# A two-level Strassen kernel: when the additions for later operands are queued

## The chip, the cores and the metric

One core of a Trainium2 chip. The metric is the device time of one execution in microseconds; the median of three runs is 793.61 (793.61 to 793.72). All times below are in microseconds unless marked otherwise.

## The reference

With a depth of one, the reference is a single gated short-convolution layer on a sequence of 1024 tokens of width 1024:

```
u = rms_norm(x, pre_norm)
z, bg, cg, v = split(u @ w_in, 4)              # w_in 1024 x 8192, four parts of 2048
y = bg * causal_dwconv(cg * v, conv_w) * silu(z)   # 3 taps over the tokens, per channel
m = y @ w_out                                  # w_out 2048 x 1024
out = x + rms_norm(m, post_norm)
```

Everything is float32.

## The kernel before

**Products.** Each float32 matrix product is made on TensorE from a rounded high part and a rest (`split`: ScalarE copies the high part, VectorE subtracts it to get the low part), as low x high, high x low and high x high. On top of that lies Strassen's scheme in Winograd's form: a 2 x 2 block product takes seven products, called a, b, c, e, d, f and g in the order in which they are issued, in place of eight. The operands of the products are sums of blocks. A product of u with w_in is `product(p, i)`: 12 matmuls of 512 columns into a bank of PSUM. Products a, c, d and g of a pair accumulate in one bank (`px`), e and f in another (`pv`). What a bank holds after a, c and e is copied to SBUF by ScalarE (`snap`, L196) before the next product adds to it, and VectorE adds the copies to later states (`after`: L215 for d, giving `sne`, L220 for f, giving `snc`).

**Pairs.** The 2048 channels go in 16 chunks of 128. Chunk c has two pairs of blocks of w_in: pair p = 2c (cg and v) and pair p = 2c + 1 (z and bg). So pairs run from 0 to 31, and the main loop does the slots of pairs 2 to 31. From pair 6 on (`DEEP = 3` chunks are done without it) product b is itself taken apart once more: the small products a' to g' work on 256 columns, and lie between the large ones. Their left operands c', e', d' and g' are sums of quarters of the operand of b. They are made once: `deep_parts(k)` puts high and low part of block k together again (L618, one addition on GpSimd for each k), `deep_subs(k)` makes four subtractions on GpSimd (L624 to L627), and `deep_split` splits one of the four sums into high and low (two ScalarE copies and two VectorE subtractions of 256 columns; `ucl_deep`, `u_b`, `udl_deep` and `ugl_deep` are the subtractions' outputs). c' is first needed behind f of pair 6.

**Beside the products.** In each pair GpSimd makes the four sums of w_in's blocks for the next pair (`add_s`: L146, L148, L142, L150), the sums for the small products (`deep_sums`, L650 to L654) and products with the gates (L217, L223, L225). VectorE makes the low parts (all at L155: `wcl` is the low part of the operand of product c), the additions after each product, and the convolution (`conv`, L583, started by `start_conv` behind g of an even pair for the first chunks, later behind d'). After f of an odd pair ScalarE takes the SiLU of `snc` (L222), after g' that of `sna` (L793).

**w_out.** The last product, y with w_out, also goes by Strassen's scheme, and the sums of w_out's blocks are made ahead of it in eight of the pairs: `fetch_t(j)` loads four blocks of 128 x 512 behind product c of the pair (L276), `add_t` subtracts them in four dependent steps on VectorE (L281 to L284) and stores each to DRAM (L286, `t_d`). `TODO` says which pair does which j. In an even pair this stands behind product d, in an odd one behind g.

**What sets the order.** The schedule is manual: every engine runs its instructions in the order in which the code issues them. One loop goes through the slots, and for each one issues the product, then `prepare` (the splits for products that start within 7.0 units; a large product counts 2.72 and a small one 0.72), then `after`, then loads, sums and the extras of that slot, last of them what the table `UNDER` names for it. All DMAs are issued by SP, which also runs in order. 36 pages of 2 KB for each partition hold all passing tiles.

Of the kernel before, what the change touches and what calls it, by code (L numbers as in the profile page):

```python
# [16 lines left out]
DEEP = 3  # L17
# [4 lines left out]
def kernel(  # L22
# [16 lines left out]
    nc = tc.nc  # L39
# [31 lines left out]
    def page(name, dtype=F32, shape=(HB,)):  # L71

        return pages.tile([P, *shape], dtype, tag="pg", name=name, bufs=PAGES)
# [58 lines left out]
    def block(p, n, k):  # L132
        return flat(raws[p, n, k])
# [19 lines left out]
    def split(src, hi, lo):  # L153
        nc.scalar.copy(hi, src)  # L154
        nc.vector.tensor_sub(lo, src, hi.bitcast(F32))  # L155
# [21 lines left out]
    def product(p, i, ks=None):  # L177

        w = wt[p, i]
        which = {"b": "y", "e": "v", "f": "v"}.get(i, "x")  # L180
        first = i in "abe"
        if first and (p, which) not in banks:
            banks[p, which] = bank(f"p{which}_{p}")
        ps = banks[p, which]
        for k in range(KH) if ks is None else ks:
            hi, lo = (h[:, k * P : (k + 1) * P] for h in w)
            last = k == KH - 1
            nc.tensor.matmul(ps, lo, UH[i][:, k], start=first and k == 0, stop=False, skip_group_check=True)  # L188
            nc.tensor.matmul(ps, hi, UL[i][:, k], start=False, stop=False, skip_group_check=True)  # L189
            nc.tensor.matmul(ps, hi, UH[i][:, k], start=False, stop=last, skip_group_check=True)  # L190
# [55 lines left out]
    def fetch_s(c):  # L246

        if c >= CH:
            ts = [page(f"s{e}_{c}") for e in (0, 1)]
            for e in (0, 1):  # L250
                nc.sync.dma_start(ts[e], y_d[:, c - CH, e * HB : (e + 1) * HB])
            done[c] = done[c], *ts
# [17 lines left out]
    ts = {}  # L270

    def fetch_t(j):

        ts[j] = [page(f"t{n}_{j}") for n in range(4)]
        for n, t in enumerate(ts[j]):
            nc.sync.dma_start(t, wov[:, j + n // 2 * CH, n % 2 * HB : (n % 2 + 1) * HB])  # L276

    def add_t(j, eng):

        t = ts.pop(j)  # L280
        eng.tensor_sub(t[1], t[1], t[0])  # L281
        eng.tensor_sub(t[3], t[3], t[1])
        eng.tensor_sub(t[0], t[3], t[0])
        eng.tensor_sub(t[2], t[2], t[3])  # L284
        for n in range(4):
            nc.sync.dma_start(t_d[:, n, j], t[n])  # L286


# [325 lines left out]
    def deep_parts(ks):  # L614

        for k in ks:
            deep[k] = page(f"deep{k}")
            nc.gpsimd.tensor_add(deep[k], UH["b"][:, k].bitcast(F32), UL["b"][:, k].bitcast(F32))  # L618

    def deep_subs(ks):  # L620

        for k in ks:
            (b11, b12), (b21, b22) = ((t[:, :HH], t[:, HH:]) for t in (deep[k], deep[k + KQ]))
            nc.gpsimd.tensor_sub(b12, b12, b11)  # L624
            nc.gpsimd.tensor_sub(b22, b22, b12)
            nc.gpsimd.tensor_sub(b11, b22, b11)
            nc.gpsimd.tensor_sub(b21, b21, b22)  # L627
# [3 lines left out]
    def deep_split(i):  # L631

        k0, l0 = DEEP_U[i]
        ls = slice(l0, l0 + HH)
        if i != "e'":
            deep[i] = [tmp.tile([P, KQ, HH], F32R, tag="ub", name=f"u{i[0]}{h}_deep", bufs=6) for h in "hl"]
        for k in range(KQ):
            if i == "e'":
                hi, lo = UH["b"][:, k, ls], UL["b"][:, k, ls]
            else:  # L640
                hi, lo = (t[:, k] for t in deep[i])
            split(deep[k0 + k][:, ls], hi, lo)

    def deep_sums(c, part):

        (a11, a12), (a21, a22) = ((t[:, :HH], t[:, HH:]) for t in (block(p, 0, 1) for p in (2 * c, 2 * c + 1)))
        t = page(f"ds{part}_{c}")
        deep[c, part] = t
        if part == 0:
            nc.gpsimd.tensor_add(t[:, :HH], a21, a22)  # L650
            nc.gpsimd.tensor_sub(t[:, HH:], t[:, :HH], a11)
        else:
            nc.gpsimd.tensor_sub(t[:, :HH], a11, a21)
            nc.gpsimd.tensor_sub(t[:, HH:], a12, deep[c, 0][:, HH:])  # L654
# [17 lines left out]
    def deep_product(c, i):  # L672

        n, off = DEEP_W[i]
        which = {"b'": "y'", "e'": "v'", "f'": "v'"}.get(i, "x'")
        first = i in ("a'", "b'", "e'")
        if first:
            banks[c, which] = bank(f"p{which[0]}2_{c}")
        ps = banks[c, which][:, :HH]
        for k in range(KQ):  # L680
            hi, lo = (h[:, off + k * P : off + (k + 1) * P] for h in deep_w[c, n])
            if i in deep:
                uh, ul = (t[:, k] for t in deep[i])
            else:
                kk, l0 = {"a'": (k, 0), "b'": (k + KQ, 0), "e'": (k, HH), "f'": (k + KQ, HH)}[i]
                uh, ul = (u["b"][:, kk, l0 : l0 + HH] for u in (UH, UL))
            nc.tensor.matmul(ps, lo, uh, start=first and k == 0, stop=False, skip_group_check=True)  # L687
            nc.tensor.matmul(ps, hi, ul, start=False, stop=False, skip_group_check=True)  # L688
            nc.tensor.matmul(ps, hi, uh, start=False, stop=k == KQ - 1, skip_group_check=True)  # L689
# [5 lines left out]
    def deep_after(c, i):  # L695
        which, row, half = DEEP_C[i]
        t = sn[2 * c + row, "a"][:, half * HH : (half + 1) * HH]
        nc.vector.tensor_add(t, banks[c, which][:, :HH], t)
        if i == "d'":
            start_conv(c)  # L700
# [34 lines left out]
        OP[side, i, h] = t  # L735

    END = len(PAIRS) - 1
    TODO = {p: j for j, p in enumerate([4, 8, 10, 12, 14, 16, 15, 17])}

    slots = [("a", 2), ("b", 2)]  # L740
    for p in range(2, len(PAIRS)):
# [14 lines left out]


    UNDER = {
        ("c", 2 * DEEP - 1): lambda: deep_parts([0, 2]),
        ("e", 2 * DEEP - 1): lambda: deep_parts([1, 3]),  # L760
        ("d", 2 * DEEP - 1): lambda: deep_subs([0]),
        ("f", 2 * DEEP - 1): lambda: deep_subs([1]),
        ("a", 2 * DEEP): lambda: deep_split("c'"),
        ("g", 2 * DEEP - 1): lambda: deep_split("e'"),
        ("c", 2 * DEEP): lambda: deep_split("d'"),
        ("e", 2 * DEEP): lambda: deep_split("g'"),
    }


    at, t = [], 0.0  # L770
# [6 lines left out]
    def prepare(n):  # L777
        while ready[0] < len(slots) and at[ready[0]] < at[n + 1] + LEAD:
            i, p = slots[ready[0]]
            if i[1:]:  # L780
                deep_prep(p, i)
            elif (p, i) not in wt:
                split_w(p, i)
            ready[0] += 1

    first_chunk("")
    for n, (i, p) in enumerate(slots):
        if i[1:]:
            deep_product(p, i)
            prepare(n)  # L790
            deep_after(p, i)
            if i == "g'":
                nc.scalar.activation(sn[2 * p + 1, "a"], sn[2 * p + 1, "a"], AF.Silu)  # L793
            continue
        product(p, i)
        prepare(n)
        after(p, i)
        q, prev = p + 1, p // 2 - 1
        if p == 2:
            first_chunk(i)  # L800
        if i == "c":
            if p % 2 and p // 2 < DEEP:
                nc.scalar.activation(sn[p, "a"], sn[p, "a"], AF.Silu)
            if p in TODO:
                fetch_t(TODO[p])
            if p % 2 == 0 and p > 2:
                fetch_s(prev)
            if p % 2 == 0 and p // 2 >= DEEP:
                deep_sums(p // 2, 1)
        elif i == "e":  # L810
            add_s(q, "ec")
        elif i == "d":
            if p + 2 <= END:
                fetch(p + 2)
            add_s(q, "d")
            if p in TODO and p % 2 == 0:
                add_t(TODO[p], nc.vector)
            if p % 2 == 0 and p > 2:
                add_y(prev)
        elif i == "f":  # L820
            add_s(q, "f")
            if p == 2:
                add_y(0)
        elif i == "g":
            if p in TODO and p % 2:
                add_t(TODO[p], nc.vector)
            if p % 2 and q <= END and q // 2 >= DEEP:
                deep_sums(q // 2, 0)
        if DEEP < NC and (i, p) in UNDER:
            UNDER[i, p]()  # L830
        if p == END - 1 and i in "cd":
            fetch_unit()
        if p == END and i in "acdg":
            split_unit()
            fetch_unit()
# [153 lines left out]
```

## Time and profile before

| | |
|---|---|
| median of three runs | 793.61 |
| the profiled execution | 793.75 |
| its span, first to last instruction | 791.9 |
| mean granted TensorE clock | 0.999 |
| busy: TensorE, weight loads, VectorE | 780.0, 654.0, 601.7 |
| busy: ScalarE, GpSimd | 335.6, 360.8 |
| pairs 2 to 31, c of pair 4 at | 103.52 |
| c of pairs 5, 6, 7, 8 at | 122.56, 139.47, 161.85, 180.36 |
| c of pairs 14, 16, 18 at | 293.70, 331.48, 370.22 |

PE is TensorE, PEld its weight loads, DVE VectorE, ACT ScalarE, POOL GpSimd, SP SyncE. A row of the timeline gives the start, the duration, the engine, the line and the operation, the written and the read tiles with their shapes, and in brackets how long the engine was idle in front of it and what ended that. A row of waits gives who waited for whom: the total, the number and the longest. A row of windows gives a stretch, its length, and the busy time of PE, PEld, DVE, ACT and POOL with the number of instructions, then the granted clock, the DMA share and GB/s.

### The profile page before, as it was taken

To read this page: it belongs to the slowest core of one execution; us is meant where nothing else is said; L and a number is where in the kernel's file an instruction comes from. 1 tells how busy PE (TensorE), PEld (TensorE's weight loads), DVE (VectorE), ACT (ScalarE), POOL (GpSimd) and SP (SyncE) were. 2 spreads that over 40 slices of the span, in tenths; PEclk is the share of its full clock that TensorE was granted. 3 is DMA by queue.
4 is the path that set the end of the run, shared out by engine and by line. 5 is a ranking of instruction groups with operands and counts; after the bars stand their busy time and mean duration, and the time that the engine had idled before them with its cause. 6 is when DMAs were issued, how large, how long until landed. Compare 5 with 4: busy or idle time off the path is not lost.

```text
span 791.9 us, 10797 instructions
## 1 busy us (share of the span) xinstructions
PE 780.0 (99%) x3728; PEld 654.0 (83%) x3728; DVE 601.7 (76%) x832; ACT 335.6 (42%) x610; POOL 360.8 (46%) x257
## 2 busy tenths in 40 slices
PE   9999999899999999999999999999999999999996
PEld 8888887788888888888888888888888888888885
DVE  6899757788787878798977768787878867744766
ACT  8564433333433343424242434242434547554441
POOL 2616538747474746555564737373838100000020
PEclk9999999999999999999999999999999999999999
DMA  9110451226161708182714233232415569973037
GB/s 328 46 53 16 132 199 55 80 66 200 54 220 34 241 12 282 51 284 75 226 56 145 87 114 106 95 106 93 144 57 169 190 207 393 403 276 118 0 108 264
DMA packets 108325, 114.50 MB, mean 145 GB/s; under 512 B 6584, under 2 KB 72176, under 8 KB 108272
## 3 DMA queue, kind: packets, MB, share of 16 engines
q1 hardware_dynamic: 108256, 113.82, 43.3%
q8 instruction: 29, 0.48, 0.2%
q14 instruction: 24, 0.20, 0.1%
q10 hardware_dynamic: 16, 0.00, 0.0%
HBM read 84.44 MB, written 29.36 MB: 144 GB/s over the span
## 4 chain that ended last, share of the span: by engine, by line
PE 80%; DVE 6%; POOL 5%; issue 4%; DMA 3%; ACT 2%; SPq 0%; DVEq 0%; POOLq 0%; ACTq 0%
PE px L188 12%; PE px L189 12%; PE px L190 11%; PE pv L188 6%; PE pv L189 6%; PE pv L190 6%; PE po_x L867 3%; PE po_x L865 3%; PE po_x L866 3%; PE po_v L867 2%; PE po_v L865 2%; PE po_v L866 2%; PE px L687 1%; PE px L689 1%; PE px L688 1%
## 5 line engine op out<-in xcount | busy, mean ns | idle before, releaser
L217 POOL TENSOR_TENSOR sne<-sne,cv 128x512 f32<-128x512 f32 x15 | 25.1, 1673 | 155.9 <-DVE sne L215 140.2
L907 POOL TENSOR_TENSOR acc<-acc,xr 128x512 f32<-128x512 f32 x4 | 6.4, 1592 | 132.8 <-DVE acc L906 130.9
L583 DVE SCALAR_TENSOR_TENSOR cv<-gpad,cw,cv 128x1024 f32<-128x1024 f32 x32 | 43.9, 1371 | 19.0 <-ACT cv L581 18.5
L146 POOL TENSOR_TENSOR se<-raw,raw 128x512 f32<-128x512 f32 x31 | 51.8, 1670 | 3.1 <-DMA raw<-in_sc_w_in 2.7
L150 POOL TENSOR_TENSOR sf<-raw,sc 128x512 f32<-128x512 f32 x31 | 53.1, 1711 | 0.0
L225 POOL TENSOR_TENSOR gpad<-snc,sne 128x512 f32<-128x512 f32 x15 | 20.2, 1345 | 71.1 <-DVE snc L220 71.1
L155 DVE TENSOR_TENSOR wel<-se,weh 128x512 fp32r<-128x512 f32 x31 | 50.9, 1641 | 1.4 <-ACT weh L154 1.4
L148 POOL TENSOR_TENSOR sc<-se,raw 128x512 f32<-128x512 f32 x31 | 50.0, 1614 | 2.4
L188 PE MATMUL pv<-u_f,wfl 128*128 128x512 f32 x124 | 48.6, 392 | 1.6 <-DVE wfl L155 1.3
L188 PE MATMUL px<-u_d,wdl 128*128 128x512 f32 x124 | 48.6, 392 | 0.0
L188 PE MATMUL px<-u_a,wal 128*128 128x512 f32 x124 | 48.6, 392 | 0.0
L188 PE MATMUL pv<-u_e,wel 128*128 128x512 f32 x124 | 48.6, 392 | 0.0
L196 ACT COPY sna<-px 128x512 f32<-128x512 f32 x30 | 17.5, 583 | 73.3 <-PE px L190 47.8
L188 PE MATMUL px<-u_g,wgl 128*128 128x512 f32 x124 | 48.5, 391 | 0.0
L189 PE MATMUL pv<-u_e,weh 128*128 128x512 f32 x124 | 48.6, 392 | 0.0
L189 PE MATMUL px<-u_d,wdh 128*128 128x512 f32 x124 | 48.6, 392 | 0.0
L189 PE MATMUL px<-u_a,wah 128*128 128x512 f32 x124 | 48.6, 392 | 0.0
L189 PE MATMUL px<-u_g,wgh 128*128 128x512 f32 x124 | 48.4, 390 | 0.0
L190 PE MATMUL pv<-u_f,wfh 128*128 128x512 f32 x124 | 48.3, 389 | 0.0
L189 PE MATMUL pv<-u_f,wfh 128*128 128x512 f32 x124 | 48.3, 389 | 0.0
L190 PE MATMUL px<-u_g,wgh 128*128 128x512 f32 x124 | 48.3, 389 | 0.0
L189 PE MATMUL px<-u_c,wch 128*128 128x512 f32 x124 | 48.2, 389 | 0.0
(370 smaller groups left out, 2484.1 us busy)
## 6 DMA issues: line engine op xcount, KB each, us to landing
raw<-in_sc_w_in SPq DMA_DIRECT2D x128, 256.0 KB, 4.2
y_d<-cv SPq DMA_DIRECT2D x16, 512.0 KB, 3.0
s_d<-s SPq DMA_DIRECT2D x32, 256.0 KB, 2.4
t<-in_sc_w_out SPq DMA_DIRECT2D x32, 256.0 KB, 4.3
t_d<-t SPq DMA_DIRECT2D x32, 256.0 KB, 2.3
s<-y_d SPq DMA_DIRECT2D x16, 256.0 KB, 3.9
xr<-in_x SPq DMA_DIRECT2D x16, 256.0 KB, 4.5
xa<-in_x SPq DMA_DIRECT2D x4, 512.0 KB, 5.4
```

The source lines that it names most:

```text
L146: nc.gpsimd.tensor_add(t, block(p, 1, 0), block(p, 1, 1))
L148: nc.gpsimd.tensor_sub(t, sums[p, "e"], block(p, 0, 0))
L150: nc.gpsimd.tensor_sub(t, block(p, 0, 1), sums[p, "c"])
L155: nc.vector.tensor_sub(lo, src, hi.bitcast(F32))
L188: nc.tensor.matmul(ps, lo, UH[i][:, k], start=first and k == 0, stop=False, skip_group_check=True)
L189: nc.tensor.matmul(ps, hi, UL[i][:, k], start=False, stop=False, skip_group_check=True)
L190: nc.tensor.matmul(ps, hi, UH[i][:, k], start=False, stop=last, skip_group_check=True)
L217: nc.gpsimd.tensor_mul(t, t, cvs[c][:, HB:])
L583: nc.vector.scalar_tensor_tensor(cv, gpad[:, j : j + L], tap(c, j), cv, op0=ALU.mult, op1=ALU.add)
L865: nc.tensor.matmul(ps, lo, u[:, 0, k], start=first, stop=False, skip_group_check=True)
L866: nc.tensor.matmul(ps, hi, u[:, 1, k], start=False, stop=False, skip_group_check=True)
L867: nc.tensor.matmul(ps, hi, u[:, 0, k], start=False, stop=last, skip_group_check=True)
```

## The change

`TODO` gives the w_out sums to pairs 8, 10, 12, 13, 14, 15, 16 and 17, where it was 4, 8, 10, 12, 14, 15, 16 and 17. In odd pairs the four steps no longer stand together behind g: one stands behind each of d, f, a (of the next pair, which is issued before g) and g, each with its store. In even pairs all four still stand behind d. `UNDER` has the work for the small products' operands earlier and in smaller pieces: the four additions behind c, e, d and f of pair 4 (before: two behind c and two behind e of pair 5), the subtractions behind g of pair 4 and c of pair 5 (before: d and f of pair 5), and the splits behind e, d and f of pair 5 and a of pair 6 (before: a of pair 6, g of pair 5, c and e of pair 6). The amount of work is the same.

```diff
-    def add_t(j, eng):
+    def add_t(j, steps=range(4)):
 
-        t = ts.pop(j)
-        eng.tensor_sub(t[1], t[1], t[0])
-        eng.tensor_sub(t[3], t[3], t[1])
-        eng.tensor_sub(t[0], t[3], t[0])
-        eng.tensor_sub(t[2], t[2], t[3])
-        for n in range(4):
+        t = ts[j]
+        for n, a, b in [((1, 1, 0), (3, 3, 1), (0, 3, 0), (2, 2, 3))[n] for n in steps]:
+            nc.vector.tensor_sub(t[n], t[a], t[b])
             nc.sync.dma_start(t_d[:, n, j], t[n])
...
-    TODO = {p: j for j, p in enumerate([4, 8, 10, 12, 14, 16, 15, 17])}
+    TODO = {p: j for j, p in enumerate([8, 10, 12, 13, 14, 15, 16, 17])}
...
     UNDER = {
-        ("c", 2 * DEEP - 1): lambda: deep_parts([0, 2]),
-        ("e", 2 * DEEP - 1): lambda: deep_parts([1, 3]),
-        ("d", 2 * DEEP - 1): lambda: deep_subs([0]),
-        ("f", 2 * DEEP - 1): lambda: deep_subs([1]),
-        ("a", 2 * DEEP): lambda: deep_split("c'"),
-        ("g", 2 * DEEP - 1): lambda: deep_split("e'"),
-        ("c", 2 * DEEP): lambda: deep_split("d'"),
-        ("e", 2 * DEEP): lambda: deep_split("g'"),
+        ("c", 2 * DEEP - 2): lambda: deep_parts([0]),
+        ("e", 2 * DEEP - 2): lambda: deep_parts([2]),
+        ("d", 2 * DEEP - 2): lambda: deep_parts([1]),
+        ("f", 2 * DEEP - 2): lambda: deep_parts([3]),
+        ("g", 2 * DEEP - 2): lambda: deep_subs([0]),
+        ("c", 2 * DEEP - 1): lambda: deep_subs([1]),
+        ("e", 2 * DEEP - 1): lambda: deep_split("c'"),
+        ("d", 2 * DEEP - 1): lambda: deep_split("e'"),
+        ("f", 2 * DEEP - 1): lambda: deep_split("d'"),
+        ("a", 2 * DEEP): lambda: deep_split("g'"),
     }
...
             if p in TODO and p % 2 == 0:
-                add_t(TODO[p], nc.vector)
+                add_t(TODO[p])
...
         elif i == "g":
-            if p in TODO and p % 2:
-                add_t(TODO[p], nc.vector)
             if p % 2 and q <= END and q // 2 >= DEEP:
                 deep_sums(q // 2, 0)
+        if i in "dfag" and p % 2 != (i == "a") and p - (i == "a") in TODO:
+            add_t(TODO[p - (i == "a")], ["dfag".index(i)])
```

## Prediction, made before the changed kernel was run

> **What bounds the kernel now.** I read the page, then TensorE's waits, then the busy time of each pair from the start of its product c to that of the next pair, then the timelines around the waits.
>
> ```profile
> span 791.9 us, 10797 instructions
> PE 780.0 (99%) x3728; PEld 654.0 (83%) x3728; DVE 601.7 (76%) x832; ACT 335.6 (42%) x610; POOL 360.8 (46%) x257
> ```
> ```profile
> PE px L687 <- DVE dw1l L155: 1.5, 1, 1.5
> PE pv L188 <- DVE wfl L155: 1.3, 2, 1.0
> PE pv L188 <- ACT wch L154: 0.3, 2, 0.2
> ```
> ```profile
> 103.52:122.56 19.04, 19.04 (x85) 15.77 (x84) 12.27 (x17) 4.88 (x9) 6.62 (x5) 1.00 0.74 241
> 122.56:139.47 16.91, 16.57 (x74) 13.44 (x72) 13.13 (x12) 7.58 (x13) 14.24 (x11) 1.00 0.09 25
> 139.47:161.85 22.38, 19.95 (x98) 16.26 (x96) 17.59 (x23) 8.78 (x19) 16.83 (x16) 1.00 0.32 94
> ...
> 293.70:312.97 19.27, 19.27 (x98) 16.37 (x97) 16.86 (x22) 6.85 (x12) 14.63 (x11) 1.00 0.71 231
> 312.97:331.48 18.51, 18.51 (x92) 15.63 (x90) 12.97 (x17) 7.37 (x13) 7.44 (x6) 1.00 0.29 88
> 331.48:351.18 19.70, 19.55 (x98) 16.29 (x96) 18.87 (x23) 6.22 (x11) 11.57 (x9) 1.00 0.68 235
> 351.18:370.22 19.04, 18.76 (x92) 15.55 (x90) 16.20 (x20) 7.99 (x14) 10.82 (x8) 1.00 0.43 130
> 370.22:389.90 19.68, 19.52 (x98) 16.29 (x96) 19.51 (x22) 6.23 (x11) 13.51 (x10) 1.00 0.60 201
> ```
>
> TensorE is busy for 99% of the span, so work on the other engines counts only where it makes or ends a wait of TensorE. The window rows (stretch and length, then PE, PEld, DVE, ACT, POOL, clock) are pairs 4, 5, 6 and 14 to 18. Pair 4 has seven products in 19.04, so one takes 2.72. An undisturbed even pair takes 19.27 and an odd one 18.51. Against these, pair 5 (six products, 16.32) loses 0.59, pair 6 loses 3.11, pair 16 0.43, pair 17 0.53 and pair 18 0.41. That is 3.70 around the preparation of the small products' operands and 1.37 around the odd pairs with w_out sums, 5.07 in all: the most that the change can win. A loss is some 0.25 more than its named wait: a product otherwise starts 0.16 before its predecessor's end, and after a wait it restarts some 0.1 slower.
>
> One mechanism prices everything here. It is seen ahead of product c of pair 16 (c16):
>
> ```profile
> 325.42 0.69 DVE L215 TENSOR_TENSOR sne<-px,sne 128x512 f32<-128x512 f32 x1
> 326.02 0.68 DVE L155 TENSOR_TENSOR wcl<-sc,wch 128x512 fp32r<-128x512 f32 x1
> 326.62 0.68 DVE L220 TENSOR_TENSOR snc<-pv,snc 128x512 f32<-128x512 f32 x1
> 327.22 0.41 DVE L698 TENSOR_TENSOR sna<-px,sna 128x256 f32<-128x256 f32 x1
> 329.03 0.69 DVE L155 TENSOR_TENSOR dw0l<-raw,dw0h 128x512 fp32r<-128x512 f32 x1 [1.40 <-ACT dw0h L154]
> 329.64 1.78 DVE L155 TENSOR_TENSOR wel<-se,weh 128x512 fp32r<-128x512 f32 x1
> ```
> ```profile
> 326.18 1.68 POOL L217 TENSOR_TENSOR sne<-sne,cv 128x512 f32<-128x512 f32 x1 [10.99 <-DVE sne L215]
> 327.83 1.29 POOL L142 TENSOR_TENSOR raw<-raw,raw 128x512 f32<-128x512 f32 x1
> 329.08 1.80 POOL L223 TENSOR_TENSOR cv<-snc,sne 128x512 f32<-128x512 f32 x1
> ```
> ```profile
> 327.33 0.63 ACT L222 ACTIVATE snc<-snc 128x512 f32<-128x512 f32 x1 [4.05 <-DVE snc L220]
> 327.87 0.62 ACT L793 ACTIVATE sna<-sna 128x512 f32<-128x512 f32 x1
> ...
> 329.42 0.58 ACT L196 COPY sna<-px 128x512 f32<-128x512 f32 x1
> ```
> ```profile
> 331.25 0.39 PE L190 MATMUL px<-u_g,wgh 128*128 128x512 f32 x1
> 331.48 0.39 PE L188 MATMUL px<-u_c,wcl 128*128 128x512 f32 x1
> ```
>
> VectorE and GpSimd take turns, one whole instruction each, when both work from SBUF. L217 waits for wcl and ends 1.16 after it; L223 ends 1.16 after dw0l; wel ends 0.54 after L223. An own turn is thus some 1.15 on GpSimd and 0.55 on VectorE (I take half of that at 256 columns), and an addition of 0.69 becomes up to 1.8 where it meets a GpSimd instruction. VectorE instructions that read PSUM are not held: snc takes 0.68 beside L217.
>
> The same rows give the chain that ends at c16: sne, wcl, snc, SiLU (L222), SiLU (L793), the first halves of the splits of dw0 and e, and the copy of a16's bank (L196). c16 accumulates in that bank and must wait for the copy. It ends at 330.00, c16 starts at 331.48: 1.48 of slack, and nobody waits today.
>
> The Trainium skill (SBUF — State Buffer, "SBUF: two separate sides") has a rule that speaks against single additions among GpSimd's work: the two engines share a port pair under an exclusive lock held for a whole instruction, VectorE's side only with two SBUF inputs. The rows agree (1.78 for wel), and add the order of turns, which the page doesn't state.
>
> **Part 1: pairs 13, 15 and 17 one by one.** Step n of the w_out sums now stands behind products d, f, a and g. Worked for pair 15: step t1 comes behind sne and takes wcl's free turn (326.02 to 326.71). L217 then ends at 327.86, wcl has to wait for it (328.41), and snc starts at 328.33 in place of 326.62 and ends at 329.01, 1.71 late. L142 takes its turn at 328.41 and ends at 329.56; step t3 waits for it and ends at 330.11; the sum sna (L698) behind t3 ends at 330.45 in place of 327.63. SiLU L793 needs sna: it starts at 330.48 in place of 327.87, 2.61 late, ACT's queue behind it moves as a whole, and the copy ends at 332.61. c16 starts at 332.65, 1.17 late, and with the slower restart 1.27 is lost. Three such pairs, ahead of c14, c16 and c18: 3.81.
>
> What these pairs win: before, four additions stood in front of the split wfl for f16.
>
> ```profile
> 334.37 1.23 DVE L281 TENSOR_TENSOR t<-t,t 128x512 f32<-128x512 f32 x1
> ...
> 339.51 1.77 DVE L155 TENSOR_TENSOR wfl<-sf,wfh 128x512 fp32r<-128x512 f32 x1
> ```
> ```profile
> 340.89 0.39 PE L190 MATMUL px<-u_d,wdh 128*128 128x512 f32 x1
> ```
> ```profile
> t<-in_sc_w_out SPq DMA_DIRECT2D x32, 256.0 KB, 4.3
> ```
>
> f16 was due at 341.12 (0.23 behind the last matmul of d16), wfl came at 341.28. Afterwards L223 ends at 331.27, L150 alone (1.29) at 332.5 and dw0l at 333.07. From there both queues alternate: six VectorE turns of 0.55 (wel, t0, wdl, L230, t2, wfl), four GpSimd turns of 0.58 and three of 1.15, 9.1 together, so wfl ends near 342.2. TensorE, 1.27 late, needs it at 342.4: no loss, 0.2 to spare. The waits of pairs 16 to 18 (1.37) go. SP's queue: an odd pair's loads are issued at c as before and first read two products later (over 5.4 us, against 4.3 to land). Each store waits on SP for its own step, and behind it stand only the next store, y_d and the next even pair's loads, a few tenths later; that pair's idle VectorE time (19.27 less 16.86) hides it, and without that cover it would cost about pair 16's 0.43. Pair 4 loses its additions; pair 13 has 5.5 idle on VectorE for its own (18.51 less 12.97). Sum of part 1: 3.81 less 1.37, 2.44 slower. Bounds: 1.37 faster if both steps find free turns (two at 0.60, inside the slack); 5.9 slower if each chain waits one more turn of 1.15.
>
> **Part 2: the small products' operands earlier.**
>
> ```profile
> 117.11 1.68 POOL L225 TENSOR_TENSOR gpad<-snc,sne 128x512 f32<-128x512 f32 x1 [12.42 <-DVE snc L220]
> ```
> ```profile
> 124.72 4.64 DVE L583 SCALAR_TENSOR_TENSOR cv<-gpad,cw,cv 128x1024 f32<-128x1024 f32 x2 [1.27 <-ACT cv L581]
> ...
> 134.23 0.69 DVE L220 TENSOR_TENSOR snc<-pv,snc 128x512 f32<-128x512 f32 x1 [0.75 <-PE pv L190]
> ...
> 144.23 0.63 DVE L155 TENSOR_TENSOR ucl_deep<-deep,uch_deep 128x256 fp32r<-128x256 f32 x1 [5.08 <-ACT uch_deep L154]
> ```
>
> Before, VectorE idles 5.08 until the subtractions are through, and the work behind it, dw1l last, comes late. Afterwards three of the four additions L618 fall into GpSimd's idle 12.42, which hides them (three turns of 1.15, 3.5; without that cover they would stand ahead of c6). Without pair 4's four additions, snc of f4 can start when TensorE ends f4 (103.52 plus 4 x 2.72 plus 0.16), so L225 starts at 115.4, and with L150 and the fourth L618 GpSimd is at 119.5. Eight subtractions of 0.7, two VectorE turns of 0.55 and the two L583 (1.1 each) bring it to 128.4; wfl for f5 ends at 128.9, due at 122.56 plus 3 x 2.72, 130.72. Pair 5's 0.59 goes.
>
> Then the new place costs. In alternation: L146 130.1, wal 130.6, L148 131.8, both ucl 132.4, wgl 133.0, sne 133.6, the first split of e' 133.9, L217 135.0, the second 135.3, L142 136.5, wcl 137.0, snc 137.6 in place of 134.9. From SiLU's start to the copy's end pair 15 takes 2.67; here the second SiLU isn't between them but two half-width copies of d' are, an estimate of 0.2 more: the copy of a6 ends at 140.4. c6 is due at 139.47 less 0.59, 138.88, and loses 1.6. From L223 (138.3) both queues alternate without a gap: GpSimd 1.29, 1.15, four of 0.58, three of 1.15; VectorE four of 0.28 and five of 0.55; 12.1 together, so wfl for f6 ends at 150.4. f6 is due 9.64 behind c6 (as f16 behind c16) at 150.1: it loses 0.6. c' no longer waits, since the splits are behind it. Part 2 loses 2.2 where before lost 3.7: 1.5 faster. Bounds: 3.7 faster if snc keeps its time; 0.8 slower if two more GpSimd turns come in front. Both queues' order is written out, so I take the worked value.
>
> **Sum.** 2.44 slower less 1.5 faster is 0.94 slower. The profiled execution took 793.75 (span 791.9, the rest around it) beside a median of 793.61: 794.6 on the median's scale. About 0.2% (1.6 us) is what a measurement here can tell from no change, so 792.0 to 795.2 is "same".
>
> **The rivals.**
> - *Relief without a bill.* The chains to c14, c16 and c18 stay inside their 1.48, because the steps find free turns. For it: two additions alone cost 1.2. Against it: L217 stands right behind sne (326.18). With part 2 as worked, 793.6 less 1.37 less 1.5 gives 790.8; with all waits gone, 788.5. It would also come about if VectorE, once it has the turn, kept it for its next instruction; against that, L217 went ahead of everything behind wcl. The Trainium skill (SBUF — State Buffer, the same section) says that whoever starts first blocks the other and no more; read so, it allows this order and 790.8. Chance 0.2.
> - *A longer bill, slower.* If L217 takes its turn before the first split of e', both splits and wcl each wait for a GpSimd turn. The copy of a6 is 1.15 later, c6 loses 2.8, f6 0.5 to 1.0, and part 2 wins 0.4 at most. It decides once c6 and f6 together lose over 2.85. With part 1 that is 793.6 plus 2.44 less 0.4, 795.7; with f14, f16 and f18 late by 0.4 each, 797. For it: f16 has only 0.2 to spare. Chance 0.36.
> - *The steps come too early for their data.* Then step t1 would hold VectorE's queue at d; 5.4 against 4.3 leaves it no chance of its own.
>
> **How the numbers follow.** The forecast has 0.44, with a range of its own of 793.2 to 795.2. Relief (0.2) is the faster side, the longer bill (0.36) the slower one. With about a tenth left out at each end the range is 790.8 to 797.0.
>
> **What would show it.** Right: in TensorE's waits a new line px L188 on ACT sna L196, four times, 1.0 to 1.5 each, ahead of c6, c14, c16 and c18; none on dw1l; in pair 15 wcl at some 1.75 in place of 0.68 and snc 1.7 later behind it; the 5.08 of idle VectorE gone. Wrong: no wait on L196 means that the steps found free turns and the kernel is faster; a pair 6 over 22 means that part 2 won nothing.

## The result, and the profile after

The changed kernel takes 796.17 (795.04 to 796.80) where the kernel before takes 793.72 (793.42 to 794.39) in the same session: ratio 1.003, interval 1.0019 to 1.0041, so 2.4 slower. The profiled execution took 795.90, its span is 794.1.

TensorE's waits in the main part of the changed kernel (who waited for whom: total, times, longest):

```profile
PE px L188 <- ACT sna L196: 4.5, 4, 1.4
PE pv L684 <- DVE sna L695: 0.6, 1, 0.6
PE pv L188 <- DVE wfl L155: 0.3, 1, 0.3
```

The first line did not exist before: four waits for the copy of a bank, 1.40 ahead of c6, 1.08 ahead of c14, 1.03 ahead of c16 and 1.02 ahead of c18. The windows of pairs 5, 6 and 13 to 18 show what they cost (stretch, length, busy PE, PEld, DVE, ACT, POOL, then the granted clock, the DMA share and GB/s):

```profile
122.46:140.33 17.87, 16.48 (x73) 13.33 (x71) 15.37 (x15) 9.04 (x19) 13.79 (x12) 1.00 0.05 13
140.33:160.33 20.00, 19.69 (x97) 16.41 (x97) 19.97 (x23) 7.83 (x15) 14.26 (x12) 1.00 0.35 107
273.67:293.43 19.76, 18.68 (x92) 15.46 (x90) 14.36 (x17) 7.01 (x13) 8.44 (x7) 1.00 0.30 94
293.43:312.88 19.45, 19.45 (x97) 16.41 (x98) 17.62 (x23) 6.49 (x12) 9.31 (x8) 1.00 0.67 216
312.88:333.42 20.54, 18.94 (x92) 15.39 (x90) 17.88 (x20) 7.53 (x14) 12.06 (x9) 1.00 0.44 142
333.42:352.89 19.47, 19.47 (x97) 16.41 (x97) 18.82 (x23) 6.49 (x12) 10.61 (x9) 1.00 0.66 228
352.89:372.59 19.70, 18.68 (x92) 15.46 (x90) 16.66 (x20) 7.63 (x14) 10.84 (x8) 1.00 0.42 135
372.59:392.07 19.48, 19.48 (x97) 16.40 (x97) 19.38 (x23) 6.94 (x13) 12.29 (x10) 1.00 0.57 190
```

Against 16.32, 18.51 and 19.27 for undisturbed pairs, pairs 5 and 6 lose 1.55 and 0.73, 2.28 where before lost 3.70: 1.42 won. Pairs 13 to 18 lose 1.25, 0.18, 2.03, 0.20, 1.19 and 0.21, 5.06 where before lost 1.37: 3.69 lost. The net of 2.3 is the difference of the spans (2.2): the rest of the kernel kept its time within 0.1.

The chain to c16 in the changed kernel, VectorE, GpSimd, ScalarE and TensorE in turn (L282 is a w_out step, L695 the sum sna, L792 the second SiLU):

```profile
326.17 0.69 DVE L215 TENSOR_TENSOR sne<-px,sne 128x512 f32<-128x512 f32 x1
326.77 0.69 DVE L282 TENSOR_TENSOR t<-t,t 128x512 f32<-128x512 f32 x1
327.37 1.78 DVE L155 TENSOR_TENSOR wcl<-sc,wch 128x512 fp32r<-128x512 f32 x1
329.08 0.68 DVE L220 TENSOR_TENSOR snc<-pv,snc 128x512 f32<-128x512 f32 x1
329.68 1.18 DVE L282 TENSOR_TENSOR t<-t,t 128x512 f32<-128x512 f32 x1
330.78 0.41 DVE L695 TENSOR_TENSOR sna<-px,sna 128x256 f32<-128x256 f32 x1
```
```profile
326.93 1.67 POOL L217 TENSOR_TENSOR sne<-sne,cv 128x512 f32<-128x512 f32 x1 [8.15 <-DVE sne L215]
328.56 1.74 POOL L142 TENSOR_TENSOR raw<-raw,raw 128x512 f32<-128x512 f32 x1
```
```profile
331.22 0.63 ACT L792 ACTIVATE sna<-sna 128x512 f32<-128x512 f32 x1 [0.80 <-DVE sna L695]
...
332.79 0.58 ACT L196 COPY sna<-px 128x512 f32<-128x512 f32 x1
```
```profile
333.42 0.50 PE L188 MATMUL px<-u_c,wcl 128*128 128x512 f32 x1 [1.03 <-ACT sna L196]
```

The first step took wcl's free turn, wcl went from 0.68 to 1.78 behind L217, and the second step took 1.18 behind L142. From sne's start to snc's start it is 2.91 where it was 1.20 (1.71 more, as worked). To the end of the copy it is 7.20 where it was 4.58: 2.62 later, worked as 2.61.

The line on L695 is the wait that the prediction did not have. It is ahead of f' in pair 15, and it begins in pair 14:

```profile
307.00 0.69 DVE L282 TENSOR_TENSOR t<-t,t 128x512 f32<-128x512 f32 x1 [0.95 <-DMA t<-in_sc_w_out]
308.50 2.02 DVE L282 TENSOR_TENSOR t<-t,t 128x512 f32<-128x512 f32 x3 [0.81 <-DMA t<-in_sc_w_out]
```
```profile
316.33 0.39 PE L684 MATMUL pv<-u_b,dw2l 128*128 128x256 f32 x1 [0.57 <-DVE sna L695]
```

VectorE waits 1.76 for pair 14's blocks of w_out; before, it did not wait for them. SP issued them 8.3 behind the start of c14; before it was 3.5, as these rows of SP's queue, before and after, show (c14 started at 293.70 and 293.43):

```profile
297.20 2.44 SPq L276 DMA_DIRECT2D t<-in_sc_w_out  x4
```
```profile
301.30 0.32 SPq L283 DMA_DIRECT2D t_d<-t  x1
301.74 1.81 SPq L276 DMA_DIRECT2D t<-in_sc_w_out  x4
```

In front of them now stands the store of pair 13's last step. SP runs in order, and that store is not issued until its step ends on VectorE, at 301.27.

Before, VectorE had idle time in pair 14 (2.41), but nearly all of it, 2.31, lay ahead of the first step, which follows sne:

```profile
300.79 0.42 DVE L698 TENSOR_TENSOR sna<-py,sna 128x256 f32<-128x256 f32 x1 [0.68 <-PE py L689]
...
303.54 0.69 DVE L215 TENSOR_TENSOR sne<-px,sne 128x512 f32<-128x512 f32 x1 [1.63 <-PE px L190]
```

In the changed kernel VectorE has no idle time between c14 and sne: the last two steps of pair 13 now run there, 1.22 and 1.78 long among GpSimd's turns.

### The profile page after: what moved, and what is told of

It reads as the page before. It is cut to its first block, busy times and chain, and to the rows that moved or that the text cites. A ratio compares the mean times of both kernels' runs of the same rounds, so it can differ in the third digit from the quotient of the medians.

```text
span 794.1 us, 10778 instructions
## 1 busy us (share of the span) xinstructions
PE 780.0 (98%) x3728; PEld 653.8 (82%) x3728; DVE 609.1 (77%) x832; ACT 334.6 (42%) x610; POOL 359.9 (45%) x257
## 4 chain that ended last, share of the span: by engine, by line
PE 82%; DVE 8%; issue 3%; POOL 2%; DMA 2%; ACT 2%; DVEq 0%; SPq 0%; ACTq 0%; POOLq 0%
PE px L188 12%; PE px L189 12%; PE px L190 12%; PE pv L188 6%; PE pv L189 6%; PE pv L190 6%; PE po_x L865 3%; PE po_x L866 3%; PE po_x L864 3%; PE po_v L865 2%; PE po_v L866 2%; PE po_v L864 2%; PE px L686 1%; PE px L685 1%; PE px L684 1%
## 5 line engine op out<-in xcount | busy, mean ns | idle before, releaser
L217 POOL TENSOR_TENSOR sne<-sne,cv 128x512 f32<-128x512 f32 x15 | 24.8, 1653 | 156.6 <-DVE sne L215 140.9
L580 DVE SCALAR_TENSOR_TENSOR cv<-gpad,cw,cv 128x1024 f32<-128x1024 f32 x32 | 41.9, 1308 | 19.0 <-ACT cv L578 18.5
L188 PE MATMUL px<-u_c,wcl 128*128 128x512 f32 x124 | 48.7, 393 | 4.5 <-ACT sna L196 4.5
L225 POOL TENSOR_TENSOR gpad<-snc,sne 128x512 f32<-128x512 f32 x15 | 20.1, 1338 | 71.6 <-DVE snc L220 71.6
L150 POOL TENSOR_TENSOR sf<-raw,sc 128x512 f32<-128x512 f32 x31 | 51.4, 1658 | 0.0
L196 ACT COPY sna<-px 128x512 f32<-128x512 f32 x30 | 17.5, 582 | 74.5 <-PE px L190 59.6
L189 PE MATMUL px<-u_g,wgh 128*128 128x512 f32 x124 | 48.5, 391 | 0.0
L189 PE MATMUL px<-u_c,wch 128*128 128x512 f32 x124 | 48.3, 390 | 0.0
L190 PE MATMUL pv<-u_f,wfh 128*128 128x512 f32 x124 | 48.3, 390 | 0.0
L190 PE MATMUL px<-u_c,wch 128*128 128x512 f32 x124 | 48.3, 390 | 0.0
```

The lines of the kernel that those rows point to most:

```text
L150: nc.gpsimd.tensor_sub(t, block(p, 0, 1), sums[p, "c"])
L217: nc.gpsimd.tensor_mul(t, t, cvs[c][:, HB:])
L580: nc.vector.scalar_tensor_tensor(cv, gpad[:, j : j + L], tap(c, j), cv, op0=ALU.mult, op1=ALU.add)
```

## The experiments

Each ran five rounds beside the kernel before; the ratio is to that kernel.

**1. Part 2 undone.** The table for the small products' operands is that of before, the rest is the change.

```diff
     UNDER = {
-        ("c", 2 * DEEP - 2): lambda: deep_parts([0]),
...
+        ("c", 2 * DEEP - 1): lambda: deep_parts([0, 2]),
...
```

> The changed kernel with the small products' operands made where they were before (part 2 undone, part 1 kept). Theory (part 2 wins some 1.4 us by ending the waits on dw1l and wfl ahead of c' and f of pair 6, part 1 costs the rest): the waits ahead of c14, c16 and c18 stay at 1.0 to 1.1 each, the wait ahead of c6 goes, those of f6 (about 1.0) and of c' (about 1.5, dw1l) return, and the kernel is 0.5 to 1.5 us slower than the changed one, about 796.9. Rival (part 2 wins nothing, it only moves the waits of pair 6): 796.2 as the changed kernel, within 0.4.

797.02, ratio 1.0034 (1.0021 to 1.0046), 3.1 over its kernel before where the change is 2.4 over.

```profile
PE px L188 <- ACT sna L196: 3.1, 3, 1.1
PE px L684 <- DVE dw1l L155: 1.4, 1, 1.4
PE pv L684 <- DVE sna L695: 1.2, 2, 1.0
PE pv L188 <- DVE wfl L155: 0.6, 1, 0.6
```

The wait ahead of c6 is gone and those of f6 and c' are back, as the theory had it. Yet c' of pair 6 starts at 153.54, 1.28 earlier than before (154.82) and nearly as early as with the change. So the theory's reason fell, and that its time (about 796.9) was met is luck: what wins around pair 6 is not the earlier table but mostly that pair 4 has lost its w_out work, the four additions with their loads and stores, the only other thing that differs from before in that stretch. The spans differ by 1.1 (795.2 and 794.1). Up to a of pair 7 it is 0.2; the rest lies ahead of f' of pairs 15 and 17, which wait 1.02 and 0.16 on sna in place of 0.57 and nothing. VectorE waits longer for w_out there (2.28 in pair 14 and 1.34 in pair 16, with the change 1.76 and 0.58); why, no run shows.

**2. All four steps behind g** in pairs 13, 15 and 17.

```diff
-        if i in "dfag" and p % 2 != (i == "a") and p - (i == "a") in TODO:
-            add_t(TODO[p - (i == "a")], ["dfag".index(i)])
+        if i == "g" and p % 2 and p in TODO:
+            add_t(TODO[p])
```

> The changed kernel with all four w_out steps of pairs 13, 15 and 17 together behind g (the one-by-one part undone, pairs and part 2 kept). Theory (the two steps ahead of the copy of a's bank make c14, c16 and c18 wait): no wait on L196 is left ahead of those three; f14, f16 and f18 lose about 0.4 each as f16 and f18 did before and f' of pairs 15 and 17 about 0.5; some 793.2. Rival (it is the fourth odd or even pair in a row, pair 13, that overloads VectorE): about as slow as the changed kernel, 796, with the waits elsewhere.

793.36, ratio 0.9991 (0.9982 to 1.0000). The three waits on L196 are gone; left are the one ahead of c6 (1.4), that ahead of f6 (0.3), three of 0.15 to 0.16 ahead of f14, f16 and f18, and two of 0.2 to 0.3 ahead of f' of pairs 15 and 17. So the places of the steps cost the loss; pair 13 as such does not.

**3. Steps behind f, a, g and g.**

```diff
-        if i in "dfag" and ...
+        if i in "fag" and p % 2 != (i == "a") and p - (i == "a") in TODO:
+            add_t(TODO[p - (i == "a")], {"f": [0], "a": [1], "g": [2, 3]}[i])
```

> The changed kernel with the w_out steps of odd pairs behind f, a, g and g in place of d, f, a and g: one step in place of two ahead of the sum sna that the copy of a's bank depends on, and none ahead of wcl. Theory (turns with GpSimd): wcl gets back its free turn (0.68), sna is 0.9 late in place of 2.6, inside the 1.48 of slack, so c14, c16 and c18 wait no longer; wfl is then late instead, f14, f16 and f18 lose about 1 each, and the time is 794 to 796. Rival (each further VectorE instruction in the chain costs its wait, whatever GpSimd does): a wait on L196 of half the size, about 0.5, stays.

795.90, ratio 1.0024 (1.0014 to 1.0033).

```profile
PE pv L188 <- DVE wfl L155: 3.8, 4, 1.2
PE px L188 <- ACT sna L196: 1.4, 1, 1.4
PE pv L684 <- DVE sna L695: 0.6, 1, 0.6
```

On L196 only c6's wait is left. Instead f14, f16 and f18 wait 1.15 to 1.16 each on wfl (f6 has the other 0.3). Ahead of c16 one step is left in the chain; it took 1.19, the copy ended 0.9 late, inside the 1.48 of slack. From dw0l to wfl VectorE and GpSimd have no idle time in this trace, and the three steps between them took 1.22 and 3.47 (two); what is put there comes out ahead of f.

**4. GpSimd's turn taken away.** The kernel leaves out the product L217 in pairs 13, 15 and 17.

```diff
             if p % 2:
-                nc.gpsimd.tensor_mul(t, t, cvs[c][:, HB:])
+            if p % 2 and p not in (13, 15, 17):
+                nc.gpsimd.tensor_mul(t, t, cvs[c][:, HB:])
```

> The changed kernel without the gate product L217 on GpSimd in pairs 13, 15 and 17 (a multiplication of the output of the z half is left out in three of sixteen chunks). VectorE's instructions are the same. Theory (wcl is held by L217's turn and the second step by L142's): wcl takes 0.68 again, the steps 0.7 each, the copy of a's bank is only 1.2 late and c14, c16 and c18 don't wait; 791 to 792. Rival (the number of instructions in the chain): the waits on L196 stay above 0.5 each, and the time is over 794.

```profile
326.20 0.68 DVE L282 TENSOR_TENSOR t<-t,t 128x512 f32<-128x512 f32 x1
326.80 0.69 DVE L155 TENSOR_TENSOR wcl<-sc,wch 128x512 fp32r<-128x512 f32 x1
327.40 0.69 DVE L220 TENSOR_TENSOR snc<-pv,snc 128x512 f32<-128x512 f32 x1
328.00 0.68 DVE L282 TENSOR_TENSOR t<-t,t 128x512 f32<-128x512 f32 x1
```

VectorE's order is that of the changed kernel. wcl is back at 0.69, the second step takes 0.68 in place of 1.18, and c14, c16 and c18 no longer wait (c6 still does, 1.4). GpSimd is idle through the whole stretch: without L217 in front of it, L142 ran earlier too, so both turns are gone at once. From sne's start to the end of the copy it is 5.60, 1.0 more than before and inside the slack. This shows the turns as the cause, not the number of instructions in the chain. The time, 793.53 (ratio 0.9993, 0.9983 to 1.0002), is above the 791 to 792 expected: f' of pairs 15 and 17 wait 0.91 and 0.54 on sna, behind VectorE's waits for w_out (3.8 in all, where the changed kernel has 2.3).

**5. The even pairs' loads ahead of the odd pair's last store.**

```diff
-            if p in TODO:
+            if p in TODO and p not in (14, 16):
                 fetch_t(TODO[p])
...
+        if i == "a" and p in (14, 16):
+            fetch_t(TODO[p])
```

> The changed kernel with the w_out loads of pairs 14 and 16 issued behind a of that pair, ahead of the odd pair's last store, in place of behind c. Theory (the wait ahead of f' of chunk 7, 0.57 on sna, comes from VectorE waiting 1.8 for these loads, which SP issued late because the store of the last step stood in front): VectorE's waits on t<-in_sc_w_out at pairs 14 and 16 go, the wait ahead of f' goes, 0.5 to 1.0 less than the changed kernel, some 795.3. Rival (VectorE is late there by its queue alone): the wait ahead of f' stays at 0.5 or more and the time at 796.

795.42, ratio 1.0015 (1.0006 to 1.0024), 1.2 over its kernel before where the change is 2.4 over. VectorE runs pair 14's four steps without a wait, and TensorE's wait on L695 is gone; those on L196 stay. From c14 to c16 it is 39.19 in place of 39.99: the late loads cost 0.8.

```profile
305.93 2.73 DVE L282 TENSOR_TENSOR t<-t,t 128x512 f32<-128x512 f32 x4
...
314.00 0.41 DVE L695 TENSOR_TENSOR sna<-pv,sna 128x256 f32<-128x256 f32 x1
```
```profile
315.54 0.28 PE L684 MATMUL pv<-u_b,dw2l 128*128 128x256 f32 x1
```

The sum that f' of pair 15 waits for ends at 314.41 here, 1.13 ahead of f'. That is all the slack, and 1.76 is more.

**6. Part 2 alone**, on the kernel before: pair 4 keeps its additions.

> The kernel before with the small products' operands moved as in the change, and nothing else: pair 4 keeps its four w_out additions, odd pairs have theirs behind g. Theory after the run with part 2 undone (most of the 1.5 won around pairs 4 to 6 comes from pair 4 losing its additions, the move itself is worth a few tenths): c6 waits about 1.7 more than in the changed kernel, around 3 named, f6 about 0.3 to 1, the stretch loses 3.5 to 4.3 as before, and the time is within 0.7 of the kernel before. Rival (the move itself wins what was predicted): 1.4 faster than before, with a wait ahead of c6 of 1.4 as in the changed kernel.

795.04, ratio 1.0015 (1.0006 to 1.0024): slower, not faster. c6 waits 2.75 and f6 not at all, and there is more behind it:

```profile
141.84 0.50 PE L188 MATMUL px<-u_c,wcl 128*128 128x512 f32 x1 [2.75 <-ACT sna L196]
...
145.12 0.63 PE L189 MATMUL px<-u_c,wch 128*128 128x512 f32 x1
145.54 0.63 PE L190 MATMUL px<-u_c,wch 128*128 128x512 f32 x1
```
```profile
141.84:146.40 4.56, 4.56 (x15) 3.66 (x16) 4.56 (x5) 1.74 (x5) 4.48 (x5) 0.65 0.00 0
```

(f' of pair 17 also waits 1.09 in this trace.) After the wait the granted clock was 0.65 over 4.6 us: matmuls start 0.42 apart in place of 0.23, and c6 to a' lose another 1.6 (4.56 at 0.35 less). Around pairs 4 to 6 this makes four cases, told by the start of a of pair 7: before 155.63, part 2 alone 156.60, pair 4 without its additions (run 1) 154.35, both (the change) 154.12. Part 2 alone loses 1.0, the missing additions alone win 1.3, both win 1.5 (starts vary by 0.1 from the head of the kernel). With c6 to a as long as in the changed kernel (13.79, a wait of 0.3 ahead of f6 included, in place of 14.76) part 2 alone would start a at 155.63, exactly as before. So by this estimate it wins and loses nothing by itself, and what it lost here is the slow clock.

**7. All four steps behind e** in odd pairs.

```diff
-        if i in "dfag" and ...
+        if i == "e" and p % 2 and p in TODO:
+            add_t(TODO[p])
```

> The changed kernel with all four w_out steps of odd pairs behind e, where VectorE idles 2.0 ahead of d' and GpSimd is idle. Theory (turns): each step takes 0.69, the chain to the copy starts at most 0.5 later, so no wait ahead of c14, c16 and c18, and wfl has no step in front of it, so none ahead of f14, f16 and f18; only pair 6's waits of the changed kernel are left; 790.5 to 791.5. Rival (the loads of w_out, issued behind c, land behind e and hold VectorE's queue ahead of the convolution): waits ahead of c14, c16 and c18 on L196 stay, 793 or more.

790.83, ratio 0.9960 (0.9948 to 0.9973). In pair 15, where VectorE waited for d' and GpSimd idles for 11.09, the four take 0.69 each:

```profile
316.47 2.74 DVE L282 TENSOR_TENSOR t<-t,t 128x512 f32<-128x512 f32 x4
319.13 0.42 DVE L695 TENSOR_TENSOR sna<-px,sna 128x256 f32<-128x256 f32 x1
```

Only c6 (1.4) and f6 (0.3) still wait.

**8. The splits behind the copy of a6 as well.**

```diff
-        ("e", 2 * DEEP - 1): lambda: deep_split("c'"),
-        ("d", 2 * DEEP - 1): lambda: deep_split("e'"),
-        ("f", 2 * DEEP - 1): lambda: deep_split("d'"),
-        ("a", 2 * DEEP): lambda: deep_split("g'"),
+        ("a", 2 * DEEP): lambda: deep_split("c'"),
+        ("e", 2 * DEEP): lambda: deep_split("e'"),
+        ("c", 2 * DEEP + 1): lambda: deep_split("d'"),
+        ("e", 2 * DEEP + 1): lambda: deep_split("g'"),
```

> As the one before, and the splits of the small products' operands spread behind the copy of a6: c' behind a of pair 6, e' behind e of pair 6, d' behind c and g' behind e of pair 7, each still ahead of its first use. Theory (the four splits ahead of snc of pair 5 cost a GpSimd turn each): snc of pair 5 starts about 2.5 earlier, the wait ahead of c6 (1.4) goes and that ahead of f6 (0.3) too, nothing of the 5.07 is left: 788.5 to 789.5. Rival (GpSimd's own queue, late by the eight subtractions, holds the sums for pair 6): the wait ahead of c6 or f6 stays at 1 or more, 790 or more.

788.36 (788.16 to 788.79), ratio 0.9930 (0.9917 to 0.9942). In the main part TensorE waits for nobody any more. snc of pair 5 starts at 133.72, when its product is through, in place of 136.81 with the change, and wcl has its free turn back:

```profile
132.27 0.68 DVE L215 TENSOR_TENSOR sne<-px,sne 128x512 f32<-128x512 f32 x1
132.87 0.68 DVE L155 TENSOR_TENSOR wcl<-sc,wch 128x512 fp32r<-128x512 f32 x1
133.72 0.69 DVE L220 TENSOR_TENSOR snc<-pv,snc 128x512 f32<-128x512 f32 x1 [0.17 <-PE pv L190]
```

It is the fastest of these kernels, 0.7% under the kernel before. The amount of work is the same; only the places of the steps and of the splits differ from the change.

## Why the prediction was right, and where it was off

**Part 1, the bill.** 3.81 was worked for c14, c16 and c18. The trace has waits of 1.02 to 1.08 and losses, restarts included, of about 1.4 each: 4.2. The chain came as written (wcl 1.78, copy 2.62 late), and the run without L217 shows the cause.

**Part 1, the gain.** The waits of f16 and f18 went, and so did that ahead of f' of pair 17. f16 came with no wait, as the ledger had it.

**The step that failed** is SP's queue: the next even pair's loads "a few tenths later; that pair's idle VectorE time (19.27 less 16.86) hides it". Both halves were wrong for pair 14. In pair 16 there was no delay at all: the odd pair's stores stood in front of its loads already, which were issued 9.0 behind c16 before and 8.4 with the change. But pair 13 had no stores before, so pair 14's loads went from 3.5 to 8.3 behind c14. And the idle time, counted in the kernel before, was no cover: it lay ahead of the loads' first use, and pair 13's two last steps took it up. VectorE waited 1.76, the slack was 1.13 (run 5), and TensorE lost 0.8 ahead of f' in pair 15. With the loads issued early (run 5) both losses are gone, which shows the cause. With the 0.4 on the bill it makes most of what separates the worked 0.94 from the 2.3 of the trace.

**Part 2** was worked as 1.5 won; the trace has 1.42, with c6 starting at 140.33 (worked 140.4) and wfl of f6 late by 0.3 (worked 0.6). The sum was right, and so was the reason that the prediction gave for the start of it: pair 4's missing additions let GpSimd begin earlier (L225 at 115.27 in place of 117.11, worked 115.4). What it did not separate is that this alone wins nearly everything, 1.3 of 1.5; by themselves the moved splits take back ahead of c6 what they win ahead of c'. Runs 1 and 6 showed that.

**The rivals.** Relief did not come in the change itself; runs 7 and 8 show that it was to be had with other places. By medians the kernel is 0.3% slower, 796.2 against the 793.2 to 795.2 that I had called the likeliest; it is inside the range only through the part set aside for the longer bill. Of that rival the sign came and not the mechanism: c6 lost 1.55, no more than worked, and f14, f16 and f18 did not wait. What came was late data. I had given late data no chance, and that rival had looked only at the odd pairs' own loads. So that the time still fell inside the range is in part luck.

## What to carry to other kernels

Where two engines take turns on whole instructions, an added instruction costs not only its own time but the turn that the next one loses: the first step here cost 0.6 of its own and 1.1 on wcl. Look for a stretch in which the other engine is idle and put all of it there, rather than spreading it evenly (run 7). Follow the chain to everything that a queue carries behind the added work, a bank's copy included, and compare its slack with the sum of turns. When work is moved to a new place, list what the DMA queue now has in front of the next loads there, and check that the idle time counted on as cover lies behind the wait and is not taken up by the moved work itself.

## What the runs showed of the hardware

TensorE waits of 1.0 to 1.5 left the granted clock at 1.00 in the windows behind them, but a single wait of 2.75 was followed by 4.6 us at a mean of 0.65, the slow part starting 1.3 after the restart, and cost 1.6 on top. The Trainium skill (TensorE: Matmul & The Clock Gate, "What's actually happening") puts the fall of the clock at an idle window of about 3.4 us. Here a shorter wait was enough, in the one run that had it. All eleven executions of that kernel have a mean granted clock of 0.993 to 0.997, those of the kernel before beside it 0.997 to 0.999.
